# Hybrid attention block on one core: a later split, a later weight cast and a weight split on another engine

## The chip, the core and the metric

The kernel runs on one core of a Trainium2 chip. The core has a matrix engine (PE, with the loading of its stationary operand shown apart as PEld), a vector engine (DVE), an activation engine (ACT), a general engine (POOL) and a queue engine (SP) that issues most of the transfers. All engines read and write one on-chip memory (SBUF); PE writes into accumulators (PSUM) that ACT and DVE read. The metric is the time of one execution on the device, in microseconds; a kernel's time is the median of its runs.

## The reference

One layer of a hybrid block is computed in float32. 16 learned tokens stand ahead of 512 input tokens (528 in all), model width 1024.

```
hn   = rmsnorm(h)
proj = hn @ w_in     # sb_q, sb_k, sb_v (512 each), g_q, g_k (512), g_v, g_r (1024), g_lr (16), merge (2048)

# stick-breaking attention, 8 heads of 64
z    = q.k / sqrt(64);  strict = key position < query position
u    = where(strict, log_sigmoid(-z), 0)
tail = cumsum of u from the right, without the element itself
w    = where(strict, exp(log_sigmoid(z) + tail), 0);   sb = w @ v

# gated linear attention, 4 heads (keys 128, values 256)
S_t = diag(exp(g_t)) S_{t-1} + k_t^T v_t;   o_t = q_t S_t;   o = rmsnorm(o) * silu(g_r)

mix = (sigmoid(merge_1) * (sb @ w_sb_out) + sigmoid(merge_2) * (o @ w_gla_out)) @ w_o
h   = h + rmsnorm(mix)
ffn = (gelu(causal_conv3(hn2 @ w_ffn_up)) * (hn2 @ w_ffn_gate)) @ w_ffn_down,   hn2 = rmsnorm(h)
h   = h + rmsnorm(ffn)
```

## The kernel before, in words

**Products from pairs.** Each float32 operand x of a large product is kept as a pair: hi, a copy of x in the matrix engine's faster float format, and lo = x - hi in the same format. A product then takes three matmuls, hi.hi, hi.lo and lo.hi. `split` (L144) makes a pair with a copy on ACT and a subtraction on DVE; `split_v` (L148) makes both on DVE.

**Weights.** `load_w` (L79) does this for a column block of weights (1024 x 128): a DMA issued by SP brings it into a tile `raw`, ACT casts it into `wh` (L88), and POOL, or another engine given as `lo_eng`, computes `wl` (L91). The pool `wp` has three buffers for `raw` and two each for `wh` and `wl`; with `into=wx` the pair lies in another pool. `proj` (L102) runs the 48 matmuls of one block: 8 slices of the depth, three products each, and two ranges of tokens, into an accumulator with the tag `mm`, of which there are two. In the traces the tiles' numbers are left out: `wh_sv`, for example, stands for each of the four blocks of values' weights `sv0` to `sv3`.

**Order.** The program is written as one stream of instructions. A planner puts each engine's instructions into an order, among those that it holds to be ready in its own model of time, earlier written ones first; on the chip each engine works its list off in that fixed order and waits where something isn't there. Tiles of one tag share a fixed number of buffers. `with tc.issue_after(x)` adds one rule: what the block issues on x's engine comes behind x in that engine's list; instructions that the block puts on other engines are not bound by it.

**Stages.** First the input norm; then the gated linear attention: for each of its 4 heads projections of keys, queries and values (`gla_proj`, L435) and the body `gla` (L459). The body ends with the gated and split output in three pieces (L608 to L619): transposes `ot` on PE, a product into `gated` on DVE, then `split` into `oh` (ACT) and `ol` (DVE); the last piece has 32 columns. After the fourth head `sb_proj(0)` (L359) is written: projections of keys, queries and values for the first two stick-breaking heads, each copied from its accumulator by ACT into `raw_k`, `raw_q`, `raw_v`, of which there is one buffer each.

Then a loop over four pairs of heads, j = 0 to 3 (L795): `sb_parts(j)` (L635) makes the pairs `ks`, `qh`, `ql` and, through transposes `svt` (accumulator tag `s`, two buffers), `vs`; `sb(j)` (L705) computes the attention; `sb_proj(j + 1)` and two `gated_gla` (L789: projections `mg` and `go`) follow. The tiles of `sb_parts` lie in a memory pool that reuses the room of `gla`'s, so they can't be written before `gla` has read its last tile there.

Inside `sb`, each head goes through the key blocks i = 2, 1, 0 (L759): `logits` into an accumulator `z`; `softplus` (ACT and DVE) into `v`; a mask on POOL; `parts` (L678, both halves on DVE: `v0h`, `v0l` for i = 0); the running sum as matmuls `z <- v0h` and `z <- v0l` with a triangular matrix (`two`, L684); and `weights` (L688): an exponential on ACT into `w`, a mask on POOL, a factor on DVE for the later columns, and again `parts` on DVE (`w1h`, `w1l` for i = 1). The pairs of weights are first used behind the loop over i, by the products `po` (L784).

**Around the second norm.** After the loop come the other gates (`gate_sb`, L807), the output projections and `w_o` (`second`, L975, for token tiles 1 to 4; `first_half`, L996), each tile's residual and norms (`gained`, `normed`) and the transposes of the normed tile (`turned`, L918), whose `split` makes `h2h` (ACT) and `h2l` (DVE). Between them the first two blocks of the up and of the gate weights are loaded (L1017, `up0`, `up1`; L1027, `ga0`, `ga1`, into `wx`). `second(4, ...)` (L1023) calls `turned(2, 0)` and `turned(2, 1)` between its matmuls. The first half of the tokens is then multiplied with both pairs of weights (L1030) while tiles 3 and 4 are still being normed. Behind it come the 22 blocks of the feed-forward part and the down projection.

Of the kernel before, what the change touches and what calls it, by code (L numbers as in the profile page):

```python
# [16 lines left out]
P = 128  # L17
D = 1024
KT = D // P
# [6 lines left out]
ALL = ((0, SPLIT), (SPLIT, T))  # L26
# [23 lines left out]
def block_kernel(ctx: ExitStack, tc: tile.TileContext, x, meta_tokens, norm_mix_pre, w_in, w_gk_up, b_gk,  # L50
# [3 lines left out]
    pe, act, dve, pool, sp = nc.tensor, nc.scalar, nc.vector, nc.gpsimd, nc.sync  # L54
# [39 lines left out]
    def cols(w, c0, n=P):  # L94
        return w[:, c0 : c0 + n].rearrange("(k p) m -> p k m", p=P)
# [6 lines left out]
    def proj(w, xh, xl, segs, name, apart=False, only=None, pt=None, by_part=False):  # L102

        wh, wl = w
        nk, m = wh.shape[1], wh.shape[2]
        (l0, l1), (_, l2) = segs
        begins = only and pt is None
        pt = mmt(f"pt_{name}") if pt is None else pt
        segs = [(pt[:m, 512 - l1 + l0 : 512], l0, l1), (pt[:m, 512 : 512 + l2 - l1], l1, l2)]
        steps = [(k, a, b) for k in range(nk) for a, b in ((wh, xh), (wh, xl), (wl, xh))]  # L110
        if by_part:
            steps = [(k, a, b) for a, b in ((wh, xh), (wl, xh), (wh, xl)) for k in range(nk)]
        segs = [segs[i] for i in only] if only else segs
        for grp in ([[s] for s in segs] if apart else [segs]):
            for n, (k, a, b) in enumerate(steps):
                for dst, lo, hi in grp:
                    last_pr[0] = pe.matmul(dst, a[:, k, :], b[:, k, lo:hi], start=n == 0, stop=n == len(steps) - 1)  # L117
        return pt if begins else pt[:m, 512 - l1 + l0 : 512 + l2 - l1]
# [22 lines left out]

    last_low = [None]

    def split(hi, lo, src):  # L144
        act.copy(hi, src)  # L145
        last_low[0] = dve.tensor_tensor(out=lo, in0=src, in1=f32(hi), op=ALU.subtract)  # L146

    def split_v(hi, lo, src):  # L148
# [210 lines left out]
    def sb_proj(j):  # L359
        r = []  # L360
        for nm, c0 in (("k", C_SBK), ("q", C_SBQ), ("v", C_SBV)):
            t = pst_.tile([P, T], F32, tag=nm, name=f"raw_{nm}{j}")
            act.copy(t, proj(load_w(cols(w_in, c0 + j * P), KT, f"s{nm}{j}"), hnh, hnl, ALL, f"s{nm}{j}"))
            r.append(t)
        return r

# [264 lines left out]
    with tc.tile_pool(name="pa", bufs=1) as pa:  # L631
# [46 lines left out]
        def parts(src, tag, nm, rows, n, shape, bufs=1):  # L678
            hi = pa.tile(shape, F32R, tag=tag + "h", name=f"{tag}h{nm}", bufs=bufs)
            lo = pa.tile(shape, F32R, tag=tag + "l", name=f"{tag}l{nm}", bufs=bufs)  # L680
            last_v[0] = split_v(hi[:rows, :n], lo[:rows, :n], src)
            return hi, lo
# [2 lines left out]
            for i in range(2):  # L685
                pe.matmul(dst, lhs, hl[i][c1], start=False, stop=False, skip_group_check=True)

        def weights(z, rows, n, nm, masks, tag, bufs, later=()):  # L688
            w = pa.tile([P, 512], F32, tag="w", name=f"w{nm}", bufs=2)
            act.activation(w[:rows, :n], z, AF.Exp)  # L690
            masks(w)
            for c, f in later:
                dve.tensor_tensor(out=w[:rows, c], in0=w[:rows, c], in1=f, op=ALU.mult)
            return parts(w[:rows, :n], tag, nm, rows, n, [P, n], bufs)

        def passed(nm, vp, rows, n, cs, tag):

# [7 lines left out]
        def sb(j, ks, qh, ql, vs):  # L705
            qk = (ks, qh, ql)
            S = slice
            o32 = pa.tile([P, T], F32, tag="o32", name=f"o32_{j}")

            zs = pst(f"zs{j}", "z")[:16, :64]  # L710
            for hd in range(2):
                for w, t in enumerate((0, 512)):
                    cc = 32 * hd + 16 * w
                    logits(zs[:, cc : cc + 16], qk, hd, S(t, t + 16), S(t, t + 16), hd == 0 and w == 0)
            v = softplus(zs, 64, 16, f"s{j}", 4)
            m16 = [[0, 4], [1, 16]]
            strict(v[:16, :64].rearrange("p (a t) -> p a t", a=4), -1, m16)
            vsp = parts(v[:16, :64], "vs", f"{j}", 16, 64, [P, 64])
            two(zs, tri[:16, :16], vsp, (S(0, 16), S(0, 64)))
            ws = weights(zs, 16, 64, f"s{j}", lambda w: strict(w[:16, :64].rearrange("p (a t) -> p a t", a=4), -1, m16), "ws", 2)  # L720
            e4 = passed(f"4{j}", vsp, 16, 64, S(0, 64), "4").rearrange("p (h w t) -> p h w t", h=2, w=2)[:, :, 1, :]


            z3 = pst(f"z3{j}", "z")[:, :288]
            for hd in range(2):
                logits(z3[:, 144 * hd : 144 * hd + 144], qk, hd, S(384, 512), S(384, 528), hd == 0)
            v3 = softplus(z3, 288, P, f"3{j}", 3)
            strict(v3[:, :288].rearrange("p (h t) -> p h t", h=2)[:, :, :P], -1, [[0, 2], [1, P]])
            v3p = parts(v3[:, :288], "v3", f"{j}", P, 288, [P, 288])
            two(z3, tri, v3p, (S(0, P), S(0, 288)))  # L730

            def mask3(w):
                w = w[:, :288].rearrange("p (h t) -> p h t", h=2)
                strict(w[:, :, :P], -1, [[0, 2], [1, P]])
                dve.tensor_tensor(out=w[:, :, P:], in0=w[:, :, P:], in1=e4, op=ALU.mult)

            w3 = weights(z3, P, 288, f"3{j}", mask3, "w3", 2)
            e3 = passed(f"3{j}", v3p, P, 288, S(0, 288), "3").rearrange("p (h t) -> p h t", h=2)
            pool.tensor_tensor(out=e3[:, :, P:], in0=e3[:, :, P:], in1=e4, op=ALU.mult)


            pm16 = pst(f"pm{j}")
            for hd in range(2):
                for i, b in enumerate(ws):
                    pe.matmul(pm16[:, 16 * hd : 16 * hd + 16], vs[:16, 0, hd, :], b[:16, 32 * hd : 32 * hd + 16], start=i == 0, stop=i == 1)

            def add_halves(hd, src, t0, n):

                lo = pa.tile([64, 512], F32, tag="lo", name=f"lo{j}_{hd}_{t0}")
                act.copy(lo[:, :n], src[64:128])  # L750
                dve.tensor_tensor(out=o32[64 * hd : 64 * hd + 64, t0 : t0 + n], in0=src[0:64], in1=lo[:, :n], op=ALU.add)

            for hd in range(2):
                add_halves(hd, pm16[:, 16 * hd : 16 * hd + 16], 0, 16)

            for hd in range(2):
                wts = []
                e = e3[:, hd, :]
                for i in (2, 1, 0):  # L759
                    t = max(i * P, NM)  # L760
                    n = T - t
                    nm = f"{i}{j}_{hd}"
                    z = pst(f"z{nm}", "z")[:, :n]
                    logits(z, qk, hd, S(i * P, i * P + P), S(t, T), True)
                    vi = softplus(z, n, P, nm, i)
                    dg = i * P + P - t
                    strict(vi[:, :dg], t - i * P - 1, [[1, dg]])
                    vp = parts(vi[:, :n], f"v{i}", nm, P, n, [P, n])
                    low = last_v[0]
                    two(z, tri, vp, (S(0, P), S(0, n)))  # L770
                    wts.append((i, t, weights(z, P, n, nm, lambda w: strict(w[:, :dg], t - i * P - 1, [[1, dg]]), f"w{i}", 1,
                                              ((S(dg, n), e),))))
                    if i:
                        en = passed(nm, vp, P, n, S(0, n), f"{i}")
                        pool.tensor_tensor(out=en[:, P:], in0=en[:, P:], in1=e, op=ALU.mult)
                        e = en

                po = pst(f"po{j}_{hd}")
                ops = [(t - NM, vs[:, i, hd, :], b) for i, t, wt in reversed(wts) for b in wt]
                ops += [(384 - NM, vs[:, 3, hd, :], b[:, 144 * hd : 144 * hd + 144]) for b in w3]  # L780
                ops += [(512 - NM, vs[:16, 4, hd, :], b[:16, 32 * hd + 16 : 32 * hd + 32]) for b in ws]
                ops.append(ops.pop(1))
                for q, (c, a, b) in enumerate(ops):
                    pe.matmul(po[:, c:], a, b, start=q == 0, stop=q == len(ops) - 1, skip_group_check=True)  # L784
                add_halves(hd, po, NM, 512)
            split_v(sbh[:, j, :], sbl[:, j, :], o32)
            last_v[0] = low
# [83 lines left out]
    with tc.tile_pool(name="pw", bufs=1) as pw:  # L871
# [148 lines left out]
        gained(3, second(3, {11: lambda: turned(1, 0), 17: lambda: turned(1, 1)}), 1)  # L1020
        m = mini()
        next(m)
        gained(4, second(4, {5: lambda: turned(2, 0), 11: lambda: turned(2, 1), 17: lambda: next(m)}), 1)  # L1023
        rs = [whole(i, sq, "mix") for i in (3, 4)]
        normed(3, rs[0])
        normed(4, rs[1])
        gas = [load_w(cols(w_gate, m * P), KT, f"ga{m}", into=wx) for m in range(2)]  # L1027

        begun, pgs_ = [], []
        for m_ in range(2):  # L1030
# [261 lines left out]
```

## Time and profile before

| what | value |
|---|---|
| time, median of 3 runs | 932.36 us (931.29 to 933.53) |
| the profiled execution's own time | 931.42 us |
| its span, first to last instruction | 929.7 us |
| PE busy | 910.6 us, 98% of the span |
| PEld, DVE, ACT, POOL busy | 90%, 67%, 53%, 38% |
| mean granted clock of PE | 0.999 |
| first projection of stick-breaking values (`pt_sv`) | from 224.05 us |
| attention of the four pairs of heads, first logits to last `po` | 246 to 460 us |

The profile lists an engine's instructions with start and length in microseconds, line, operation, the tiles out <- in, and the shapes. A bracket at a row's end gives the idle time of the engine before it and what ended that. The chain of waits is followed back from the last instruction, or from a window's end. Merged rows carry a count (x2).

### The profile page before, as it was taken

To read this page: it belongs to the slowest core of one execution; us is meant where nothing else is said; L and a number is where in the kernel's file an instruction comes from. 1 tells how busy PE (TensorE), PEld (TensorE's weight loads), DVE (VectorE), ACT (ScalarE), POOL (GpSimd) and SP (SyncE) were. 2 spreads that over 40 slices of the span, in tenths; PEclk is the share of its full clock that TensorE was granted. 3 is DMA by queue.
4 is the path that set the end of the run, shared out by engine and by line. 5 is a ranking of instruction groups with operands and counts; after the bars stand their busy time and mean duration, and the time that the engine had idled before them with its cause. 6 is when DMAs were issued, how large, how long until landed. Compare 5 with 4: busy or idle time off the path is not lost.

```text
span 929.7 us, 17750 instructions
## 1 busy us (share of the span) xinstructions
PE 910.6 (98%) x7156; PEld 833.6 (90%) x7156; DVE 620.6 (67%) x1074; ACT 493.9 (53%) x938; POOL 351.8 (38%) x257
## 2 busy tenths in 40 slices
PE   7999999999999999999999998999999999999997
PEld 7999999999999998989998678999999999988885
DVE  6685858586559786888647347454444445578997
ACT  7674747565566665767663245533333333255664
POOL 4433332323355453545545332644444444100200
PEclk9999999999999999999999999999999999999999
DMA  7222222222222222222224642333333333274933
GB/s 219 61 65 79 57 68 70 70 70 68 70 69 69 68 64 74 68 68 70 57 66 128 226 137 92 114 91 92 93 94 101 98 92 91 92 249 169 248 110 129
DMA packets 129875, 93.38 MB, mean 100 GB/s; under 512 B 4080, under 2 KB 114930, under 8 KB 129794
## 3 DMA queue, kind: packets, MB, share of 16 engines
q1 hardware_dynamic: 126178, 82.55, 29.8%
q10 hardware_dynamic: 2112, 6.82, 1.9%
q0 software_dynamic: 1504, 2.88, 1.8%
q8 instruction: 56, 0.92, 0.4%
q14 instruction: 25, 0.20, 0.1%
HBM read 88.05 MB, written 4.19 MB: 99 GB/s over the span
## 4 chain that ended last, share of the span: by engine, by line
PE 91%; DVE 4%; ACT 2%; SPq 1%; issue 1%; DMA 0%; POOL 0%; DVEq 0%; POOLq 0%; ACTq 0%
PE pt_up L117 13%; PE ga L965 13%; PE pt_gr L117 5%; PE pt_gv L117 5%; PE pt_mg L117 5%; PE pt_ms L117 5%; PE pt_go L117 5%; PE dA L1138 3%; PE dB L1138 3%; PE dD L1138 3%; PE pt_sv L117 3%; PE pt_sk L117 3%; PE pt_gq L117 3%; PE wo L1001 2%; PE wob L980 2%; PE pt_gk L117 2%
## 5 line engine op out<-in xcount | busy, mean ns | idle before, releaser
L91 POOL TENSOR_TENSOR wl_ga<-raw_ga,wh_ga 128x1024 fp32r<-128x1024 f32 x22 | 55.1, 2508 | 74.2 <-ACT wh_ga L88 56.9
L91 POOL TENSOR_TENSOR wl_up<-raw_up,wh_up 128x1024 fp32r<-128x1024 f32 x22 | 52.9, 2407 | 77.5 <-ACT wh_up L88 77.5
L117 PE MATMUL pt_up<-h2h,wh_up 128*128 128x256 f32 (+1 forms) x352 | 73.1, 283 | 1.3 <-ACT h2h L145 1.3
L117 PE MATMUL pt_up<-h2l,wh_up 128*128 128x256 f32 (+1 forms) x352 | 73.4, 283 | 0.0
L117 PE MATMUL pt_up<-h2h,wl_up 128*128 128x256 f32 (+1 forms) x352 | 73.2, 282 | 0.0
L965 PE MATMUL ga<-h2h,wh_ga 128*128 128x512 f32 (+1 forms) x192 | 72.0, 376 | 0.7 <-ACT h2h L145 0.7
L965 PE MATMUL ga<-h2h,wl_ga 128*128 128x512 f32 (+1 forms) x192 | 72.2, 376 | 0.0
L965 PE MATMUL ga<-h2l,wh_ga 128*128 128x512 f32 (+1 forms) x192 | 72.1, 376 | 0.0
L88 ACT CAST wh_up<-raw_up 128x1024 fp32r<-128x1024 f32 x22 | 23.1, 1049 | 77.7 <-PE pt_up L117 75.3
L117 PEld LDWEIGHTS pt_up<-h2h,wh_up 128*128 128x128 f32 x352 | 56.7, 189 | 3.3 <-ACT h2h L145 1.6
L117 PEld LDWEIGHTS pt_up<-h2l,wh_up 128*128 128x128 f32 x352 | 55.5, 189 | 0.0
L117 PEld LDWEIGHTS pt_up<-h2h,wl_up 128*128 128x128 f32 x352 | 55.4, 189 | 0.0
L965 PEld LDWEIGHTS ga<-h2h,wl_ga 128*128 128x128 f32 x192 | 36.2, 188 | 7.0
L965 PEld LDWEIGHTS ga<-h2h,wh_ga 128*128 128x128 f32 x192 | 36.1, 188 | 7.0 <-ACT h2h L145 0.9
L965 PEld LDWEIGHTS ga<-h2l,wh_ga 128*128 128x128 f32 x192 | 36.1, 188 | 6.2
L1069 DVE SCALAR_TENSOR_TENSOR cy<-pt_up,cw,cy 128x511 f32<-128x511 f32 (+1 forms) x22 | 16.4, 746 | 36.3 <-ACT cy L1066 36.3
L88 ACT CAST wh_ga<-raw_ga 128x1024 fp32r<-128x1024 f32 x22 | 23.1, 1049 | 27.2 <-PE ga L965 24.9
L1069 DVE SCALAR_TENSOR_TENSOR yp<-pt_up,cw,yp 128x511 f32<-128x511 f32 (+1 forms) x22 | 16.4, 745 | 29.7 <-ACT yp L1066 29.7
L1166 POOL DMA_DIRECT2D tv<-in_w_ffn_down_dram x6 | 7.0, 1173 | 68.4 <-DVE wl_p L146 68.4
L91 POOL TENSOR_TENSOR wl_gr<-raw_gr,wh_gr 128x1024 fp32r<-128x1024 f32 x8 | 19.1, 2388 | 33.8 <-ACT wh_gr L88 33.8
L145 ACT CAST sh_p<-As 128x512 fp32r<-128x512 f32 (+1 forms) x30 | 17.3, 583 | 22.4 <-PE dB L1138 8.1
L117 PE MATMUL pt_gr<-hnh,wh_gr 128*128 128x258 f32 (+1 forms) x128 | 28.2, 294 | 0.0
(575 smaller groups left out, 3126.8 us busy)
## 6 DMA issues: line engine op xcount, KB each, us to landing
raw_up<-in_w_ffn_up_dram SPq DMA_DIRECT2D x22, 512.0 KB, 3.9
raw_ga<-in_w_ffn_gate_dram SPq DMA_DIRECT2D x22, 512.0 KB, 3.9
raw_t<-in_w_ffn_down_dram SPq DMA_DIRECT2D x10, 512.0 KB, 7.6
raw_gv<-in_w_in_dram SPq DMA_DIRECT2D x8, 512.0 KB, 4.0
raw_gr<-in_w_in_dram SPq DMA_DIRECT2D x8, 512.0 KB, 3.8
raw_mg<-in_w_in_dram SPq DMA_DIRECT2D x8, 512.0 KB, 3.8
raw_go<-in_w_gla_out_dram SPq DMA_DIRECT2D x8, 512.0 KB, 4.0
raw_ms<-in_w_in_dram SPq DMA_DIRECT2D x8, 512.0 KB, 3.8
```

The costliest lines, as they stand in the source:

```text
L88: act.copy(hi_out, raw)
L91: lo_eng.tensor_tensor(out=lo_out, in0=raw, in1=f32(hi_out), op=ALU.subtract)
L117: last_pr[0] = pe.matmul(dst, a[:, k, :], b[:, k, lo:hi], start=n == 0, stop=n == len(steps) - 1)
L145: act.copy(hi, src)
L965: last_mm[0] = pe.matmul(pt[:, lo:hi], a[:, k, :], b[:, k, lo:hi], start=lo == 0 and k == 0 and q == 0, stop=k == KT - 1 and q == 2, skip_ ...
L980: last_mm[0] = pe.matmul(pt, a, b, start=q == 0, stop=q == len(ops) - 1)
L1001: last_mm[0] = pe.matmul(pos[i // 2][:, (i % 2) * 512 : (i % 2) * 512 + 512], m[k][:, t], w, start=k == 0 and q == 0, stop=k == 7 and q == 2)
L1069: dve.scalar_tensor_tensor(out=y[:, d:], in0=pt[:, : SEQ - d], scalar=c, in1=y[:, d:], op0=ALU.mult, op1=ALU.add)
L1138: mm[i] = pe.matmul(dsts[i], a, b, start=first and k == 0 and j == 0, stop=last and k == NP - 1 and j == 2, skip_group_check=True)
L1166: return lambda n, q, nk: pool.dma_start(out=t[:, q : q + nk, :], in_=block(s, c, q, nk), accum_op=ALU.add)
```

## The change

It has three parts.

First, in `sb`, the pair of weights of the second key block (i = 1) is no longer split as soon as its weights are ready. `weights(..., split=False)` returns a function; for i = 0 it is called under `issue_after(low.ins)`, where `low` is the subtraction that makes `v0l`. DVE therefore makes `w1h` and `w1l` behind `v0h` and `v0l`. This concerns all four pairs of heads and both heads of each.

Second, in `sb_proj(0)`, the load of the values' weights `sv0` is put under `issue_after(last_split[0].ins)`. `last_split` is the ACT copy of the latest `split` that has been written; at this place that is the copy `oh` of the last piece (32 columns) of the fourth `gla`. Bound is the one ACT instruction of the block, the cast `wh_sv0`.

Third, the load of `ga1` is put behind the ACT copy `h2h` of `turned(2, 1)` (`parts2`), again by its cast alone, and its low part is computed on DVE and not on POOL.

```diff
     def split(hi, lo, src):
-        act.copy(hi, src)
+        last_split[0] = act.copy(hi, src)
         last_low[0] = dve.tensor_tensor(out=lo, in0=src, in1=f32(hi), op=ALU.subtract)
...
-            act.copy(t, proj(load_w(cols(w_in, c0 + j * P), KT, f"s{nm}{j}"), hnh, hnl, ALL, f"s{nm}{j}"))
+
+            with tc.issue_after(last_split[0].ins) if nm == "v" and not j else ExitStack():
+                w = load_w(cols(w_in, c0 + j * P), KT, f"s{nm}{j}")
+            act.copy(t, proj(w, hnh, hnl, ALL, f"s{nm}{j}"))
...
-        def weights(z, rows, n, nm, masks, tag, bufs, later=()):
+        def weights(z, rows, n, nm, masks, tag, bufs, later=(), split=True):
...
-            return parts(w[:rows, :n], tag, nm, rows, n, [P, n], bufs)
+            both = lambda: parts(w[:rows, :n], tag, nm, rows, n, [P, n], bufs)
+            return both() if split else both
...
                     low = last_v[0]
+                    if not i:
+
+                        with tc.issue_after(low.ins):
+                            i1, t1, both = wts.pop()
+                            wts.append((i1, t1, both()))
                     two(z, tri, vp, (S(0, P), S(0, n)))
                     wts.append((i, t, weights(z, P, n, nm, lambda w: strict(w[:, :dg], t - i * P - 1, [[1, dg]]), f"w{i}", 1,
-                                              ((S(dg, n), e),))))
+                                              ((S(dg, n), e),), split=i != 1)))
...
-        gained(4, second(4, {5: lambda: turned(2, 0), 11: lambda: turned(2, 1), 17: lambda: next(m)}), 1)
+        p4 = second(4, {5: lambda: turned(2, 0), 11: lambda: turned(2, 1), 17: lambda: next(m)})
+        parts2 = last_split[0]
+        gained(4, p4, 1)
...
-        gas = [load_w(cols(w_gate, m * P), KT, f"ga{m}", into=wx) for m in range(2)]
+        gas = [load_w(cols(w_gate, 0), KT, "ga0", into=wx)]
+        with tc.issue_after(parts2.ins):
+            gas.append(load_w(cols(w_gate, P), KT, "ga1", into=wx, lo_eng=dve))
```

More of the change, by code (lines that the diff above doesn't have):

```diff
@@ L142, in block_kernel @@
     last_low = [None]
+    last_split = [None]
     def split(hi, lo, src):
-        act.copy(hi, src)
+        last_split[0] = act.copy(hi, src)
         last_low[0] = dve.tensor_tensor(out=lo, in0=src, in1=f32(hi), op=ALU.subtract)
```

## The prediction

> **What bounds the kernel now.** I read the page first, then the waits of the matrix engine, then the chain of waits and the timelines where those waits lie. The page and the waits:
>
> ```profile
> PE 910.6 (98%) x7156; PEld 833.6 (90%) x7156; DVE 620.6 (67%) x1074; ACT 493.9 (53%) x938; POOL 351.8 (38%) x257
> ```
> ```profile
> PE z L686 <- DVE v0l L150: 2.4, 2, 1.4
> PE pt_up L117 <- ACT h2h L145: 1.3, 1, 1.3
> PE zs L663 <- ACT qh L649: 0.9, 1, 0.9
> ```
>
> PE is busy for 98% of the span, so an edit gains only what it takes from PE's idle time, and loses what it adds to it. After the start three waits stand out, one near each edit: 2.4 us in two places for `v0l` (first edit), 0.9 us for `qh` at the start of the first attention (second edit), 1.3 us for `h2h` (third edit). If all three went and nothing came instead, 4.6 us would be gained. The chain before the second:
>
> ```profile
> 238.65 1.05 ACT wh_sv L88
> ...
> 239.85 2.37 DVE ol L146
> ...
> 246.60 0.59 ACT raw_k L363
> 247.24 2.21 PE pt_sv L117 x16
> ```
>
> A values' cast stands ahead of the last `oh`; its low part on POOL then holds the last `ol`, 32 columns wide, for 2.37 us; `ks`, `qh` and the copy `raw_k` follow. The question is whether the edit moves this cast. It doesn't:
>
> ```profile
> 216.18 1.04 ACT L88 CAST wh_sv<-raw_sv 128x1024 fp32r<-128x1024 f32 x1
> ...
> 232.47 0.59 ACT L363 COPY raw_v<-pt_sv 128x528 f32<-128x528 f32 x1
> ...
> 239.61 0.21 ACT L145 CAST oh<-gated 128x32 fp32r<-128x32 f32 x1
> ```
>
> The first `wh_sv` of the trace, at 216.18, belongs to `sb_proj(0)`; its projection ends with the copy `raw_v` at 232.47. The cast at 238.65 is the second, of `sb_proj(1)`, which the condition leaves alone. The edit puts the cast of 216.18 behind the `oh` of 239.61, some 20 us later in ACT's list.
>
> **The second edit, which decides.** Could PE do the projections of `sb_proj(1)` meanwhile? Their casts need the same two `wh` buffers, and whether a later tile may take a buffer ahead of an earlier one of its tag is seen elsewhere in the trace, at the third pair of heads:
>
> ```profile
> 308.78 0.58 ACT L363 COPY raw_v<-pt_sv 128x528 f32<-128x528 f32 x1
> ...
> 344.28 0.49 ACT L702 ACTIVATE E<-s 128x400 f32<-128x400 f32 x1
> ...
> 357.57 0.50 PE L784 MATMUL po<-w0l,vs 128*128 128x512 f32 x1
> 357.90 0.60 PE L655 MATMUL svt<-ident,raw_v 128*128 128x128 f32 x4
> ```
>
> `svt` reads only `raw_v`, there since 309.4, and needs one of the two `s` accumulators, both free from 344.8 until `po`. It is written before the projections that PE does in that time. Still it comes only behind the last `po` that is written before it and has the same tag. So I take it that buffers of a tag go out in written order: no `wh` tile behind `sv0` is cast before `wh_sv0`, and PE has no projection until then. What is left to it:
>
> ```profile
> 224.00:247.20 23.20, 22.13 (x181) 20.97 (x180) 12.98 (x23) 11.77 (x23) 7.16 (x3) 1.00 0.25 69
> ```
> ```profile
> 227.37 0.28 PE L581 MATMUL po<-Sh,ql 128*16 128x256 f32 x1
> ...
> 229.42 1.23 DVE L599 TENSOR_TENSOR ob<-ob,a_o 128x1024 f32<-128x1024 f32 x1
> ...
> 233.22 1.03 PE L613 MATMUL ot<-ident,ob 128*128 128x128 f32 x8
> ```
>
> The table of windows gives PE 22.13 busy of 23.20 us between the start of `pt_sv` and the point 247.2 (the columns are length, then busy time and count of PE, PEld, DVE, ACT, POOL, then clock and transfers). About 2.5 us of it is `gla`'s tail, which stays where it is: 12 products `po` of about 0.12 us and the transposes `ot`, 1.0. So 19.6 us must follow the restart R, and the kernel stands (R + 19.6) - 247.2 later.
>
> R: the tail itself speeds up on an empty PE. `ob` is ready at 230.65 but `ot` starts at 233.22, behind matmuls of the next projection: 2.6 us. The last `po` stand behind matmuls of `pt_sv`: about 2 us, an estimate from the timeline. And `oh` at 239.61 no longer waits for the cast of 238.65: about 1.1. So `oh` comes at 239.6 - 5.7 = 233.9, and with 1.05 for the cast R = 235.0: the edit costs 235.0 + 19.6 - 247.2 = 7.4 us, the old wait for `qh` already counted as gone. Bounds: if the 2 us are 2.2, R is 234.8 (7.2 us). If the tail doesn't speed up at all, R is 239.6 + 1.05 = 240.7, and if PE also waits for the low part (2.57, row below), 243.2: 15.6 us. I take 7.4, near the lower end, since the two larger terms are waits that the trace shows behind matmuls which will be missing, and the 32 products with the high part need no low one.
>
> What moves with the cast: the low part on POOL, 48 matmuls, the copy `raw_v`, `svt` and `vs`, which only the output products at the end of a head need; all beside the work above. The DMA of `sv0` stays in SP's queue, but its `raw` buffer, one of three, stays taken until about 237.6 (cast and low part done); the transfer of `sv1` waits for that, and its use is three projections behind the restart, at about 247 + 7: hidden. On ACT the copies `ks` and `qh` of the first attention stand behind the cast and wait 1 us for it; they come some 6 us earlier than now anyway. The attention gains those, but PE's backlog, not the attention, sets the end.
>
> Then the clock. PE would be nearly idle for some 9 us. The trace has no such pause later than its start; there it shows
>
> ```profile
> 1.81 4.64 PE L233 MATMUL warm<-ident 128*128 128x128 f32 x20 [1.81 <-POOL ident masks.py:199]
> ...
> 12.19 1.50 PE L233 MATMUL warm<-ident 128*128 128x128 f32 x12
> ```
>
> 20 equal matmuls in 4.6 us against 12 in 1.5: at the start each takes nearly twice as long, for at least 4.6 us, which costs 2.3 us. A restart after the pause costs between 0 and 2.3; I take 2.0, near the one row there is. [...]
>
> **The first edit.** DVE and POOL at one of the two places:
>
> ```profile
> 346.77 0.99 DVE L149 CAST v0h<-v 128x512 fp32r<-128x512 f32 x1
> 347.68 2.76 DVE L150 TENSOR_TENSOR w1l<-w,w1h 128x400 fp32r<-128x400 f32 x1
> 350.37 0.68 DVE L150 TENSOR_TENSOR v0l<-v,v0h 128x512 fp32r<-128x512 f32 x1
> ```
> ```profile
> 347.44 2.57 POOL L91 TENSOR_TENSOR wl_sv<-raw_sv,wh_sv 128x1024 fp32r<-128x1024 f32 x1
> ```
>
> `w1l` started behind POOL's subtraction and ended 0.43 behind its end (350.44 against 350.01). With the edit `v0l` stands in its place and reads two SBUF tiles likewise: it would end at about 350.0 + 0.7 = 350.7 against 351.05. That is 0.35 at this place and as much at the other, not the 2.4 of the waits. [...] Nothing is added or removed; `w1h` and `w1l` come later on DVE, ahead of `po`, which has microseconds to spare. And the second edit moves projections against the attention, so that these two meetings may fall elsewhere. I take -0.4, between -2.4 (both waits gone) and +1.0 (one more such meeting).
>
> **The third edit.**
>
> ```profile
> 560.77 1.03 ACT L88 CAST wh_ga<-raw_ga 128x1024 fp32r<-128x1024 f32 x1
> 561.70 0.59 ACT L145 CAST h2h<-ht 128x512 fp32r<-128x512 f32 x1
> ```
> ```profile
> 563.53 1.15 DVE L893 TENSOR_TENSOR mix<-sq 128x1 f32<-128x1 f32 x1
> ```
> ```profile
> 559.96 4.70 POOL L91 TENSOR_TENSOR wl_ga<-raw_ga,wh_ga 128x1024 fp32r<-128x1024 f32 x2 [17.37 <-PE wo L1001]
> ```
>
> The cast that goes behind was `ga1`'s; the `h2h` for which PE waits 1.3 us comes up to 0.9 earlier, and so do the squares behind it. POOL loses 2.35 us, so `mix`, one column in 1.15 us while POOL was busy, falls to about 0.15. DVE gets a subtraction of 128x1024, about 1.23 by the row of `ob`, in the stretch in which it norms tiles 3 and 4 for PE. I take -0.8: the wait less what is lost again at tiles 3 and 4; bounds -2.3 (wait and `mix`) and +1.2 (DVE's whole subtraction lands on the path).
>
> **The sum.** 7.4 + 2.0 - 0.4 - 0.8 = +8.2 us on the profiled execution's 931.42, so 939.6; the median of the runs, 932.36, lies 0.9 above that execution: 940.5.
>
> **Rivals.**
> - Buffers go out by readiness, and keys and queries of `sb_proj(1)` overtake `sv0`. Against it: the late `svt`. Both `mm` accumulators then fill and PE stands from about 238.7, where the second of them is full, until `raw_k` may be copied. Without a cast ahead of `oh` (1.1) and POOL work beside `ol` (2.2 of its 2.37) that is 3.3 earlier than 246.6, at 243.3: 4.6 idle against 1.1 now, +3.5, less 1.2 for the other edits: 934.7, at the edge of 0.2%.
> - The other side: the same overtaking, and the 4.6 us of the tail (2.6 and 2) are gained too, because the planner puts `ot` and `po` ahead of the keys' matmuls. Then `raw_k` is copied at 243.3 - 4.6 = 238.7 and PE never stops: -1.1 for the second edit, -2.4 and -1.3 for the others: 927.6. It decides from a copy before 239.8, where the idle time is today's.
> - Slow and more: no speed-up of the tail, and PE waits for the low part: 15.6 + 2.3 - 1.2 = +16.7: 949. The matmuls that stand ahead of `po` and `ot` in today's list speak against it.
>
> **How the numbers follow.** Forecast 0.66, little or no speed-up of the tail (944 and up) 0.14, overtaking alone 0.08 (0.05 of it within 0.2%), overtaking with the tail's gain 0.12. The range 934 to 947 holds the forecast with its bounds and part of the slower case. 0.2%, 1.9 us, is about what a measurement of this kernel can tell from no change: faster 0.12, within 0.05, slower 0.83; the forecast's own range is 936 to 944.
>
> **What would show it.** The first `wh_sv` behind the 32-column `oh`; no `pt_sk` between `pt_sq` and the first `pt_sv`; PE busy for about a quarter of the stretch 224 to 235; the second pair's `wh_sk` later than that cast. Right for the first edit: `v0l` ahead of `w1h` eight times, some of them 2.5 us long. For the third: `wl_ga` once on DVE and `h2h` ahead of the cast. The prediction is wrong if a second `pt_sk` runs before the first `pt_sv`, or if PE is full there.

## The result, and the profile after

| | before | after |
|---|---|---|
| time, median (lowest to highest) | 931.85 us (931.29 to 933.53) | 944.02 us (943.46 to 944.62) |
| span of the profiled execution | 929.7 us | 942.1 us |
| mean granted clock | 0.999 | 0.991 |

The change makes the kernel slower: the ratio is 1.0122, 95% interval 1.0109 to 1.0135. Forecast were +8.2 us on the profiled execution; its span grew by 12.4. The direction and the place were right, and 4.2 us were missing.

The page of the changed kernel, its row of busy time, and the table of PE's waits (total, times, longest):

```profile
PE 916.0 (97%) x7156; PEld 837.2 (89%) x7156; DVE 614.1 (65%) x1075; ACT 494.6 (52%) x938; POOL 343.7 (36%) x256
```
```profile
PE pt_sv L117 <- ACT wh_sv L88: 4.6, 1, 4.6
PE ot L618 <- DVE ob L604: 3.0, 1, 3.0
...
PE ht L936 <- DVE h2l L148: 1.3, 1, 1.3
...
PE po L795 <- DVE w0l L152: 1.0, 1, 1.0
PE z L691 <- DVE v0h L151: 0.9, 2, 0.8
PE z L691 <- DVE v0l L152: 0.9, 1, 0.9
PE po L795 <- DVE w0h L151: 0.8, 1, 0.8
```

PE is busier by 5.4 us than before, for the same 7156 products, and has 7.6 us of new waits at the top of its list. More busy time for equal work is a sign to look at the clock. The timeline where these two waits lie:

```profile
225.34 0.28 PE L586 MATMUL po<-Sh,ql 128*16 128x256 f32 x1
...
228.67 2.29 PE L618 MATMUL ot<-ident,ob 128*128 128x128 f32 x10 [3.05 <-DVE ob L604]
...
234.31 0.22 ACT L147 CAST oh<-gated 128x32 fp32r<-128x32 f32 x1 [1.05 <-DVE gated L623]
234.44 1.04 ACT L88 CAST wh_sv<-raw_sv 128x1024 fp32r<-128x1024 f32 x1
235.38 1.04 ACT L88 CAST wh_sk<-raw_sk 128x1024 fp32r<-128x1024 f32 x1
...
235.53 0.81 PE L117 MATMUL pt_sv<-hnh,wh_sv 128*128 128x272 f32 x2 [4.57 <-ACT wh_sv L88]
...
237.97 0.81 PE L117 MATMUL pt_sv<-hnh,wl_sv 128*128 128x272 f32 x2 [0.24 <-POOL wl_sv L91]
...
240.78 0.64 PE L117 MATMUL pt_sv<-hnh,wl_sv 128*128 128x272 f32 x2
...
243.09 0.40 PE L117 MATMUL pt_sv<-hnh,wh_sv 128*128 128x272 f32 x2
```

The last `oh` came at 234.31 where 233.9 was forecast, PE went on at 235.53 where 235.0 was, and the second pair's `wh_sk` stands directly behind the first `wh_sv`: the tail of the last head does run some 5 us faster on an empty PE, and nothing overtakes. The last two rows are pairs of products of the same shape, 0.64 at 240.78 and 0.40 at 243.09. Windows of the granted clock (third figure from the end) show why:

```profile
224.00:228.00 4.00, 1.62 (x13) 0.91 (x11) 2.46 (x9) 2.05 (x7) 0.00 (x0) 1.00 0.00 0
228.00:232.00 4.00, 2.29 (x10) 1.86 (x10) 2.35 (x5) 0.59 (x1) 0.00 (x0) 0.56 0.00 0
232.00:236.00 4.00, 0.47 (x2) 0.47 (x3) 1.68 (x4) 2.30 (x4) 0.45 (x1) 0.50 0.00 0
236.00:240.00 4.00, 3.76 (x17) 3.44 (x17) 2.98 (x2) 3.92 (x7) 4.00 (x2) 0.50 0.17 44
...
242.00:243.00 1.00, 1.00 (x10) 1.00 (x9) 0.94 (x3) 0.00 (x0) 0.00 (x0) 0.95 0.80 211
```

The clock is at one half from 228.45 to 242.1, 13.65 us: it falls in the first pause (3.05 us), stays down through the second (4.57 us), and comes back 6.6 us behind the restart.

### The profile page after: what moved, and what is told of

Its sections match the earlier page's. It is cut to its first block, busy times and chain, and to the rows that moved or that the text cites. A ratio compares the mean times of both kernels' runs of the same rounds, so it can differ in the third digit from the quotient of the medians.

```text
span 942.1 us, 17756 instructions
## 1 busy us (share of the span) xinstructions
PE 916.0 (97%) x7156; PEld 837.2 (89%) x7156; DVE 614.1 (65%) x1075; ACT 494.6 (52%) x938; POOL 343.7 (36%) x256
## 4 chain that ended last, share of the span: by engine, by line
PE 88%; DVE 5%; issue 3%; ACT 3%; POOL 1%; DMA 0%; DVEq 0%; POOLq 0%; ACTq 0%
PE pt_up L117 13%; PE ga L976 13%; PE pt_gr L117 5%; PE pt_gv L117 5%; PE pt_ms L117 4%; PE pt_mg L117 4%; PE dA L1153 3%; PE dD L1153 3%; PE dB L1153 3%; PE pt_go L117 3%; PE pt_sv L117 3%; PE pt_so L117 3%; PE wob L991 3%; PE pt_gq L117 2%; PE wo L1012 2%
## 5 line engine op out<-in xcount | busy, mean ns | idle before, releaser
L91 POOL TENSOR_TENSOR wl_ga<-raw_ga,wh_ga 128x1024 fp32r<-128x1024 f32 x21 | 53.0, 2525 | 74.7 <-ACT wh_ga L88 74.7
```

The lines of the kernel that those rows point to most:

```text
L91: lo_eng.tensor_tensor(out=lo_out, in0=raw, in1=f32(hi_out), op=ALU.subtract)
```

## The experiments

Times moved by 1 us or less are near what the runs can tell, so the traces are compared too. Executions already differ by up to 2.5 us at the last `pl` of the last head (209.8 before), ahead of anything that the change touches; therefore every shift below is counted from there. The table gives, against before, how much later PE starts its first `pt_sv` (224.05 before) and its last `wob` (556.1 before, just ahead of the third edit's place), how long the clock was at half between 224 and 250, and the ratio of the times with its interval.

| kernel | first `pt_sv` | last `wob` | half clock | ratio |
|---|---|---|---|---|
| all three edits | +11.7 | +12.0 | 13.65 us | 1.0122 (1.0109 to 1.0135) |
| edits 1 and 2 | +11.2 | +10.8 | 10.24 | 1.0114 (1.0100 to 1.0128) |
| edit 2 | +11.2 | +9.5 | 10.24 | 1.0103 (1.0090 to 1.0116) |
| edit 2, pauses filled | +11.2 | +8.5 | 0 | 1.0094 (1.0079 to 1.0110) |
| edit 2, high part first | +11.2 | +9.2 | 10.24 | 1.0093 (1.0079 to 1.0107) |
| edit 2, own weight buffers | +12.1 | +7.0 | 13.65 | one run |
| values written later | +16.5 | +6.1 | 6.83 | 1.0054 (1.0042 to 1.0067) |
| edit 1 | 0.0 | -0.2 | 0 | 1.0000 (0.9991 to 1.0008) |

**The edits one by one**, each with its own hunks of the change's diff and no others. The first alone:

> The first edit alone (the second weights' split behind the first softplus parts), nothing else changed. On record is -0.4 us. After the result there are two accounts of 1.8 us more that PE waits between 247 and 493 of the changed kernel's span. Theory A: the edit by itself moves nothing measurable, the 1.8 comes from the second edit, which shifts the projections against the attention, so that the subtractions on DVE and POOL meet elsewhere: this kernel is within 0.6 us of before (931.9). Rival B: the new order of the parts itself costs it, since w1h and w1l now stand behind v0l on DVE and ahead of w0h: this kernel is 1.8 us slower (933.7), with waits of PE at po for w0h or w0l that the kernel before doesn't have.

932.45 us against 932.54: theory A holds, alone it moves nothing. In its profiled execution the waits for `v0l` fall from 2.4 to 1.0 us, and as much comes back elsewhere (0.2 more for `v0h`):

```profile
PE z L688 <- DVE v0l L152: 1.0, 1, 1.0
...
PE po L792 <- DVE w0h L151: 0.7, 1, 0.7
...
PE zs L688 <- DVE vsh L151: 0.5, 1, 0.5
```

The second alone:

> The second edit alone (the first values' weight cast behind the last oh). On record is +7.4 for the pause and +2.0 for the clock. The changed kernel's trace has 6.8 us more idle time of PE between 224 and 247 and a clock of 0.50 from 228.7 to 242.0, which costs 3.3 us of the 6.5 us of projections behind the restart. Theory A: 10.1 us of pause and clock, and the 1.8 us of later waits too, because they come from the shift: +11.9, 943.8. Rival B: the later waits belong to the first edit: +10.1, 942.0. If neither, and it is +7.4 to +8.5, then the half clock costs little and the edits add up in another way.

942.06 us, +9.5; by the ratio 8.4 to 10.8. That is rival B's figure. Its reason holds in part: the first edit costs nothing by itself, and something beside the second, as the run of both below shows. The forecast for this edit, 7.4 and 2.0, was 9.4. The third alone:

> The third edit alone (the second gate weight's cast behind the second tile's casts, its low part on DVE). On record is -0.8. In the changed kernel PE's work stands 0.9 us earlier at the first up projection and gives 1.2 back at 586, where y's second half on DVE stands behind the reduction of msffn and this behind the transposes. Theory: the same happens without the other edits, +0.3 us, 932.2. Rival: the loss at 586 is one of the shifted times and not of this edit's list; then 0.9 stays, 931.0.

932.85 us, ratio 1.0004 (0.9996 to 1.0013): nothing measurable; the 0.9 doesn't stay.

**The first two together.** The edits are those of the change without its third.

> The first and second edit together, without the third. The second alone measured 942.1 against 932.5 before (+9.6), the first alone 0.0, the third alone +0.3, all three +12.2 on their chip. Theory A: the first edit, which is neutral on the schedule of before, costs about 1.3 us on the shifted one, since v0l ahead of w1h makes w0h and w0l come later where PE already waits for them at po: 943.4. Rival B: the edits add up, the rest of the +12.2 is the clock (in the changed kernel's trace the half clock lasted 13.65 us and with the second edit alone 10.24) and the chip: 942.0 to 942.5.

944.1 us. The intervals of this ratio and of the second edit's overlap, so the times don't decide. The traces differ: 10.8 against 9.5 us at the last `wob`, with the same restart and the same 10.24 us of half clock. PE's waits in the attention, first with the second edit alone, then with both:

```profile
PE po L789 <- DVE w0h L151: 3.1, 2, 1.7
...
PE z L691 <- DVE v0l L152: 0.6, 1, 0.6
```
```profile
PE po L795 <- DVE w0l L152: 1.0, 1, 1.0
PE z L691 <- DVE v0h L151: 0.9, 2, 0.8
...
PE z L691 <- DVE v0l L152: 0.9, 1, 0.9
PE po L795 <- DVE w0h L151: 0.8, 1, 0.8
```

Three waits become five of nearly the same sum (3.7 and 3.6 us). At 404 in the changed kernel a wait took more of PE's time than the gap shown: products there are listed with 0.28 us each and start 0.12 apart, and across the wait the step from one to the next was 1.15 us, 1.03 more than usual, where the gap is 0.87. From the first `zs` to the last `wob`, with the clock at full speed throughout, the two kernels with both edits take 322.6 us each; the second edit alone takes 321.3, and with its pauses filled or overfilled (below) 321.4 and 321.8. So theory A is right in direction, by two executions against three: beside the second edit the first costs 0.8 to 1.3 us. The listed waits don't account for all of it, and which subtraction costs what isn't settled. The rest of the 12.0 is the clock: with all three edits it was at half for one more stretch of 3.41 us, and the last `wob` came 1.2 later.

**The pauses filled.** Products that nothing reads, put behind the last `po` and the last `ot`:

```
+ if nm == "v" and not j:
+     for nf, aft in ((22, last_po), (34, last_ot)):
+         f = pst(f"fill{nf}", "z")
+         with tc.issue_after(aft[0].ins):
+             for _ in range(nf):
+                 pe.matmul(f[:, :P], ident, ident, start=True, stop=True)
```

> The second edit alone as in the run of the values only, with products of ident with itself (128x128, as at the kernel's start) put into PE's two pauses: 22 behind the last po, 34 behind the last ot, into accumulators that nothing reads. They take 0.125 us each at full clock, 2.75 and 4.25 us, a little less than the pauses of 3.1 and 4.6. Theory (the restart at half clock is a cost of its own, caused by the idle time): the clock stays at 1.00, the transposes run at full clock, the restart comes 0.5 earlier, and the kernel is 3.3 to 3.8 us faster than the one with the second edit alone, about 940. Rival (the clock falls for another reason, or the slow stretch hides behind waits that come anyway): no difference to the second edit alone beyond 0.6 us.

944.59 us: a miss, by my sizes. Each product is two passes in the trace (x44 and x68, 0.115 us apart); 22 and 34 filled not 2.75 and 4.25 but 5.07 and 7.86 us, and the first `pt_sv` came 4.5 us later than with the second edit alone (counted from the last `pl`). What it shows is that the clock then stays at 1.00 in this stretch. With 12 and 18:

> The second edit alone with products of ident put into PE's two pauses, now 12 and 18 of them. In the run before each product showed up as two passes of 0.115 us, so that 22 and 34 made 5.07 and 7.86 us and put the restart off by 3.2 us instead of filling the pauses of 3.1 and 4.6; its clock stayed at 1.00 there. 12 and 18 are 2.76 and 4.14 us. Theory: with the clock held the restart is no later, the 5.1 us at half clock behind it (236.5 to 241.6) cost 2.55 less and the transposes 0.3: 2.8 us faster than the second edit alone, 939.2. Rival: the slow stretch was hidden behind later waits; then 941.5 to 942.5.

940.79 us. The restart is where it was and the clock never falls, but PE is only 1.0 us earlier at the last `wob`, neither the 2.8 of the theory nor nothing (by the ratios 0.8, and their intervals overlap). The reason is in its waits:

```profile
PE pt_sv L117 <- POOL wl_sv L91: 0.7, 1, 0.7
...
PE pt_sv L117 <- ACT wh_sv L88: 0.5, 1, 0.5
...
PE pt_sk L117 <- ACT wh_sk L88: 0.2, 1, 0.2
```

At full speed PE runs into the weights that are still being split; at half speed it arrives later and waits only 0.24 for `wl_sv`. Of the 2.55 us that 5.1 us at half clock behind the restart take away (an estimate, half of 5.1), more than half was time in which PE would have waited.

**The low part.** The order of the products within the projection, for the first values alone:

```
- steps = [(k, a, b) for k in range(nk) for a, b in ((wh, xh), (wh, xl), (wl, xh))]
+ steps = [(k, a, b) for a, b in ((wh, xh), (wh, xl), (wl, xh)) for k in range(nk)]
```

> The second edit alone, with the first values' projection in another order of products: the 32 with the weight's high part first, the 16 with its low part last. The prediction counted on these 32 to cover POOL's subtraction, but the projection goes by slices of the weight, two high products and a low one each, so that PE needed the low part after 4 of the 256 and 272 wide products and waited 0.24 us and slowed what was beside. Theory: the wait for wl_sv goes, 0.5 us less than with the second edit alone up to the first zs, and the pt_sk's that filled in move behind: 0.3 to 0.8 us faster than 942.1. Rival: the low part's wait was covered by the second pair's keys, no difference (within 0.2 us in the trace at pt_ms).

PE goes through all 48 products with no wait between them:

```profile
236.39 3.88 PE L118 MATMUL pt_sv<-hnh,wh_sv 128*128 128x272 f32 x16 [4.59 <-ACT wh_sv L88]
240.07 2.77 PE L118 MATMUL pt_sv<-hnl,wh_sv 128*128 128x272 f32 x16
242.68 2.11 PE L118 MATMUL pt_sv<-hnh,wl_sv 128*128 128x272 f32 x16
```

The first `zs` comes 0.9 us earlier than with the second edit alone. Some 0.5 of that is work that only moved: four products of the second pair's keys, of 0.12 us each at full clock, now come behind it. At the last `wob` 0.3 is left, at the end 0.5. By the ratios the kernel is 0.9 us faster than with the second edit alone, where the theory had 0.3 to 0.8, but the intervals overlap. So the wait for the low part is real and, in this slow stretch, worth some 0.3 us.

**Who holds the second pair.** The first values' weight in buffers of its own:

```
- w = load_w(cols(w_in, c0 + j * P), KT, f"s{nm}{j}")
+ w = load_w(cols(w_in, c0 + j * P), KT, f"s{nm}{j}", into=own[0] if nm == "v" and not j else None)
```

> The second edit alone, with weight buffers of its own (high and low part) for the first values, so that the casts of the second pair's keys and queries needn't wait for it. In the program's order these two casts now stand ahead of the last oh. Theory (accumulators too go out in written order): PE's first pt_sk of the second pair still comes only behind the first pt_sv, PE stands from about 227 to 230 and 231.6 to 236 as with the second edit alone, the clock falls to half, and the time is that of the second edit within 1.5 us (941 to 943.5); what is gained is at most the wait for the second pair's low parts behind the restart. Rival (only the weight buffers held the second pair): pt_sk runs from 227 on and the time is 933 to 936.

The casts moved ahead and PE stood all the same:

```profile
226.32 1.05 ACT L88 CAST wh_sq<-raw_sq 128x1024 fp32r<-128x1024 f32 x1 [0.35 <-issue]
227.28 0.59 ACT L370 COPY raw_q<-pt_sq 128x528 f32<-128x528 f32 x1
```
```profile
231.60 2.29 PE L620 MATMUL ot<-ident,ob 128*128 128x128 f32 x10 [3.51 <-DVE ob L606]
238.46 0.81 PE L117 MATMUL pt_sv<-hnh,wh_sv 128*128 128x272 f32 x2 [4.57 <-ACT wh_sv L88]
...
239.51 0.64 PE L117 MATMUL pt_sk<-hnh,wh_sk 128*128 128x272 f32 x2
```

The second pair's keys and queries are cast (the queries' at 226.32) and both accumulators are free after the copy at 227.28, but `pt_sk` starts only behind `pt_sv`. So the weight buffers were not all that held it. That accumulators, too, go out in the order in which they are written would explain it; this run can't tell that from the planner's order of PE's list. With 940.93 us, one run, it came out just below the range that I gave: the second pair's low parts are ready at the restart.

Now the values' projection is written later, and the staging buffers of keys and queries are doubled:

```
+ kq0, kq1 = sb_proj(0, "kq"), sb_proj(1, "kq")
+ kqv = kq0 + sb_proj(0, "v", True)        # True: cast behind the last oh
```

> The kernel before, with the cast of the first values' weight behind the last oh as in the second edit, but also written later: the projections are written in the order keys 0, queries 0, keys 1, queries 1, values 0, and the staging of keys and queries has two buffers each, so that the copies of keys 1 and queries 1 needn't wait for the casts of keys 0 and queries 0. Theory (weight buffers and accumulators of one tag go out in written order, and that alone let PE stand): keys 1 and queries 1 fill the pause, PE is full from 224 to 240, the clock stays, and the tail of the last head no longer waits for a values' cast: 1.7 us of waits at 245 to 247 go: 930 to 931. Rival (what holds PE is the tail of the last head, the engines ACT and DVE, whatever is written first): a pause as in the second edit, 938 or more. Second rival: the keys' and queries' matmuls stand ahead of ot and oh comes late: the first attention starts later than now, 932 to 935.

938.09 us: the first rival's figure (938 or more), but not its pause: the theory's mechanism shows, and PE is full up to 239.8. But the tail runs no faster behind those products, as the second rival said:

```profile
240.32 0.22 ACT L147 CAST oh<-gated 128x32 fp32r<-128x32 f32 x1
240.44 2.00 ACT L88 CAST wh_sv<-raw_sv 128x1024 fp32r<-128x1024 f32 x2
```
```profile
241.54 0.81 PE L117 MATMUL pt_sv<-hnh,wh_sv 128*128 128x272 f32 x2 [1.75 <-ACT wh_sv L88]
```

`oh` at 240.32 is 239.4 on the clock of before, against 239.61 there and 234.5 with the change: a full PE costs the tail those 5 us. The projection then waits 1.75 for its cast, the clock falls for 6.83 us, and the first attention, which needs these values only later but the casts `ks` and `qh` behind `wh_sv` at once, starts 4.2 us later. The +6.1 in the table includes some 1.7 us, an estimate (half of 3.41), from a further stretch at half clock, 3.41 us long from 364.16.

**Two versions around the tail and the gate.** The second values' cast, the one that does hold `oh`, bound behind it, alone:

```
+ if not j:
+     last_oh[0] = last_split[0]
...
+ with tc.issue_after(last_oh[0].ins) if nm == "v" and j == 1 else ExitStack():
+     w = load_w(cols(w_in, c0 + j * P), KT, f"s{nm}{j}")
```

> The kernel before with the cast of the second values' weight, the one at 238.65 that holds the last oh, bound behind that oh, instead of the first values' cast. By the prediction's reading of the tail: oh comes 1.1 earlier, its low part isn't held by POOL's subtraction for 2.2, the copy raw_k comes up to 3.3 earlier, and PE's waits of 1.7 us between 245 and 247 go: 930.2 to 930.9. Rival: the cast lands ahead of ks or qh instead and holds these for the same 1.05 us: within 0.5 us of before.

932.5 us, ratio 0.9994 (0.9985 to 1.0003): the rival's time, though another wait is the reason. The first `zs` is 1.0 earlier, but the next ones wait 1.3 us for `ql`, whose cast takes 2.53 us on DVE beside POOL's next subtraction, `wl_mg` (the one at 244.23, with POOL idle, takes 0.43); 0.3 is left at the last `wob`. The third edit's first half:

```
+ with tc.issue_after(parts2.ins):
+     gas.append(load_w(cols(w_gate, P), KT, "ga1", into=wx))
```

> The first half of the third edit: the second gate weight's cast behind the second tile's casts, its low part left on POOL. Theory: the 0.9 us at the first up projection are the cast's and stay as with the whole edit; mix is held by POOL's second subtraction again (1.15 instead of 0.15), and y's halves stand ahead of the reduction in this list, so that the loss at 586 is smaller: PE's work stands 0.5 to 0.9 earlier behind the transposes than before. Rival: the loss comes from binding the cast, it is the same 1.1 to 1.2 as with the whole edit.

934.39 us, one run, too little for a ratio; its profiled execution also has a stretch at half clock behind the transposes (last section). In the trace the rival holds, at another place than I expected. PE starts `pt_up` 0.95 us earlier and has lost it at the last `ht`. The waits there, with the binding alone, and in the kernel before:

```profile
PE ht L927 <- DVE mssffn L950: 1.4, 1, 1.4
...
PE pt_up L117 <- ACT h2h L147: 0.4, 1, 0.4
```
```profile
PE pt_up L117 <- ACT h2h L145: 1.3, 1, 1.3
...
PE ga L965 <- ACT h2h L145: 0.7, 1, 0.7
```

With the cast bound, the third tile's first transposes and `msffn` stand behind all products of the gate's half (from 575.00) instead of amid them (from 573.41 before), so whatever hangs on them is late. With the whole third edit DVE's list differs as well, here in the changed kernel:

```profile
584.91 0.16 DVE L139 SCALAR_TENSOR_TENSOR a_ffn<-a_ffn,r_ffn 128x1 f32<-128x1 f32 x1
586.36 0.17 DVE L959 TENSOR_REDUCE mssffn<-msffn 128x2 f32<-128x16 f32 x1 [1.28 <-PE msffn L957]
586.45 1.41 DVE L927 SCALAR_TENSOR_TENSOR y<-hb,a_ffn,g2bc 128x512 f32<-128x512 f32 x2
```

DVE waits 1.28 us for `msffn` with the fourth tile's `y` ready behind it. The third edit, the second values' cast of above, and that reduction moved (`last_y` is the last `y` written):

```
+ with tc.issue_after(last_y[0].ins) if nm == "ffn0" else ExitStack():
      dve.tensor_reduce(out=ss, ...)
```

> The third edit with one more binding, the reduction of msffn on DVE behind both halves of the fourth tile's y, and the second values' cast behind the last oh (of which the trace showed -0.3 us). No first or second edit. Theory: what the third edit loses at 586 comes from that reduction, for which DVE waited 1.3 us with y ready behind it; with it moved the 0.9 gained at the first up projection stays to the end: -0.9 -0.3 = -1.2 us, 931.5 where before is 932.7. Rival: the transposes of the third tile, now behind all products of the gate's half, bring the loss whatever DVE does: within 0.4 us of before.

931.34 us against 932.33, ratio 0.9989 (0.9979 to 0.9998): 1.0 us faster than before, near the theory's 1.2 but at the edge of what can be told. At the last `ht` 0.8 of the 0.9 are still there, at `dA` 0.4.

## Why the prediction was right, and where it fell short

By the runs, in the order of the sum (the clock and the pause are separated by the filled kernel; each figure is from one execution, and adding the edits one upon another assigns what they share):

| term | forecast | measured | from |
|---|---|---|---|
| pause of PE | +7.4 | +8.5 | edit 2, pauses filled |
| clock | +2.0 | +2.2 | 9.5 - 8.5, and 12.0 - 10.8 for the stretch more |
| first edit | -0.4 | +1.3 | 10.8 - 9.5 |
| third edit and what follows | -0.8 | +0.6 | last `dA` +12.6, less 12.0 |
| sum | +8.2 | +12.6 | less 0.2 at the start: 12.4 |

- **Which cast moves, written order, the tail on an empty PE**: right, each shown by a run or the trace; the signs that were named are there too (`v0l` ahead of `w1h` eight times, `wl_ga` once on DVE, PE busy for 3.9 of the 11.0 us from 224 to 235, a third where about a quarter was named). The restart was forecast 10.95 later than the old start of `pt_sv`; it came 11.2 later with the second edit alone, and 11.7 with all three, where the clock fell earlier, ahead of the transposes `ot` (228.45).
- **The pause, 1.1 too small.** The step that failed is "the 32 products with the high part need no low one". The projection takes two high products and a low one for each slice, so PE needed `wl_sv` after the first slice's high products. The filled kernel waits 0.7 for it at full clock, and the run with the high part first has no such wait; 0.3 more is the later restart. That makes 1.0 of the 1.1; waits in the attention change as well (2.4 us for `v0l` before, 3.0 for `w0h` and 0.6 for `v0l` in the filled kernel), so this split is a reading, not a measurement of each part.
- **The clock, right in sum by luck.** I took a fixed price from the start. What it cost here did not follow its length alone: 10.24 us at half cost 1.0, since PE would have waited for part of them anyway (0.7 us for `wl_sv` at full clock, 0.24 at half), and 3.41 more cost another 1.2.
- **The first edit, mis-sized by 1.7, the largest part.** The waits for `v0l` were meant to shrink by 0.35 each. Alone the edit gives 0.0, since as much is waited for `w0h`, `vsh` and `v0h` as is saved at `v0l`, and on the schedule that the second edit shifts it costs 1.3. The prediction said that the meetings may fall elsewhere and put +1.0 as the upper end, which the 1.3 passes; it should not have taken a gain from two meetings that another edit moves.
- **The third edit.** The 0.9 at `h2h` came as forecast. What wasn't seen is that a binding on one cast also reorders PE's transposes and DVE's list 14 us later, and the gain goes there.
- **The rivals.** Overtaking was priced at 934.7, with a gain on the tail at 927.6. When the keys and queries were let ahead, by writing the values later, the kernel took 938.1: a full PE keeps the tail slow, and the cast still comes last. A time of 944 and up was foreseen for a tail that hardly speeds up; the kernel came to 944.0 although the tail did speed up, because all four terms of the sum came out above the forecast.

## What to carry to other kernels

A weight's cast moved behind a chain is worth nothing if what PE could do meanwhile takes its buffers and accumulators from the same tags and is written later: look for the written order first, then fill the pause with real work or don't make one. Gains read from waits where two engines happen to meet don't survive another edit that shifts the schedule, and one bound instruction can reorder lists far behind it; after each such edit compare the lists, not only the wait that was meant.

## What the hardware showed

Away from the two ends of the span, every stretch at half clock in these traces lasted 3.41, 6.83, 10.24 or 13.65 us: one to four times 3.41. Two rows of the run with the gate's cast bound alone, where 1.8 us without products in 3.5 were followed by one such stretch:

```profile
576.00:579.50 3.50, 1.72 (x12) 1.31 (x13) 3.21 (x11) 2.10 (x6) 0.00 (x0) 1.00 0.00 0
579.50:583.00 3.50, 3.50 (x19) 3.50 (x18) 1.06 (x3) 0.59 (x1) 0.00 (x0) 0.51 0.02 5
```

The second row costs some 1.7 us, an estimate (half of 3.41), with PE busy throughout. The idle time of PE ahead of such a stretch differs. In the 3.41 us ahead of it, 1.5 us without products were once enough (values written later, before 241.28), and so were 1.27 (third edit alone, before 354.06), while 1.75 us were once not (edit 2 alone, from 301.53, with the clock at 1.00 from 300 to 310). So the idle time does not decide alone; what else does stays open. The waits of before, 0.9 to 1.4 us each, lie near these figures: the first edit alone and the second values' cast lost one such stretch near 564 in their profiled executions (clock 0.95 from 560 to 565 and 0.71 from 565 to 570 with the first edit alone), behind a wait that the profiled execution of before has too, without loss (1.00 from 560 to 570), and the one at 354 lies ahead of all that the third edit changes.

What surprised most is that a slow clock behind a pause was mostly hidden: at half speed PE waited 0.24 us for its weights' low part, at full speed 0.7.
